# Gated embedding of a float32 encoder block: the last round of weight splits moved from GpSimd to VectorE, two squares left to the small matmuls, and one set of diagonals issued later

## The chip, the cores and the metric

One core of one Trainium2 chip. The metric is the device time of one execution, in microseconds (us): 2531.17 us for the kernel before, the median of three runs (2530.97 to 2533.29). Below, PE is TensorE (matmuls), DVE is VectorE, ACT is ScalarE, POOL is GpSimd, SP is the engine that issues most DMAs.

## The reference

The whole block has two SwiGLU half steps, two token mixers, a gated embedding and a final norm, on 1024 tokens of 1024 channels. Only its end matters here:

```python
ple_gate = jax.nn.sigmoid(rmsnorm(h, ple_norm[layer]) @ ple_w_gate[layer])
h = h + ple_gate * (p[layer] @ ple_w_proj[layer])
return rmsnorm(h, final_norm)
```

`ple_w_gate` is 1024 x 1024, `ple_w_proj` is 256 x 1024, `p` is 1024 x 256, everything in float32.

## The kernel before

**Layout.** Channels lie on the 128 partitions, tokens along the row. `h` is 8 blocks (`j`) of 128 channels by 1024 tokens, held as two halves of 512 tokens (`hsrc`, tile `r`). A float32 product is made of three passes of 32-bit "r" matmuls: each operand is split into `hi` (ACT copies and rounds, L98 for weights) and `lo` (the rest, a subtraction, L99), and `mm3` (L355) sums hi x hi, hi x lo and lo x hi.

**Weights.** `Weights` streams each 128 x 1024 unit of weights by DMA into one of four raw buffers (`wraw`, L80) and splits its two halves into one of seven slots (`wsplit`). A slot comes free when the unit that used it is done (`done`), and the next half is split at once (`ahead`). The subtraction L99 runs on the engine given to `plan`, on POOL where none is given.

**The embedding (`ple`).** The tokens are three pieces: piece 0 is tokens 0 to 511, piece 1 tokens 512 to 767, piece 2 tokens 768 to 1023. The first round (r = 0) goes through all eight blocks with pieces 0 and 1. The last round (r = 1) goes through the blocks from 7 down to 0 with piece 2 alone, and streams the gate weights of blocks 5 to 0 (and one unit of `ple_w_proj`) a second time; those of blocks 7 and 6 are kept.

A unit (one block, one piece; L1600 to L1626) is 24 gate matmuls and 6 projection matmuls on PE, then a chain: DVE L1614 (times the norm factor), ACT L1615 (sigmoid), DVE L1616 (times the projection), DVE L1618 (added into `h`), ACT L1624 (square), and one addition L1626 into the piece's sum of squares, on DVE in the last round.

**The final norm (`final`).** Per piece: `factors` sums the squares over the partitions with one small matmul per 128 tokens (L1639) and runs eleven tiny DVE instructions of a reciprocal square root (L373 to L379); `spread` makes a diagonal matrix per 128 tokens on DVE (L1650), multiplies it by ones on PE (L1651) and copies the result out of PSUM on ACT (L1653); `apply` scales each of the eight blocks, on DVE (L1668), or for blocks 1 and 5 on ACT and POOL (L1665, L1666), and stores it.

**The order.** Engines work their own queues in order. The norms of pieces 0 and 1 run inside the last round: `self.queue` holds their steps, and `tick`, called after every 8 gate matmuls (so three times per unit), takes one step from it, or counts down a number that stands there. A step's instructions are pinned behind what its engines had been given by then (`paced`). The norm of piece 2 comes after the last unit, with nothing beside it.

Of the kernel before, what the change touches and what calls it, by code (L numbers as in the profile page):

```python
# [9 lines left out]
ALU = mybir.AluOpType  # L10

P = 128
# [199 lines left out]
class Block:  # L212
# [1351 lines left out]
    def ple_plan(self):  # L1564
        io = self.io
        o = []
        for j in range(8):
            o.append((("ple", 0, j), io["ple_w_gate"][j]))
            if j % 4 == 0:
                o.append((("proj", 0, j // 4), io["ple_w_proj"][j // 4]))  # L1570
        for j in reversed(range(8 - PLE_KEPT)):
            o.append((("ple", 1, j), io["ple_w_gate"][j]))
            if j == 3:
                o.append((("proj", 1, 0), io["ple_w_proj"][0]))
        self.w.plan(o)

    def ple_keys(self, r, j):

# [14 lines left out]
    def ple(self):  # L1593

        nc, w = self.nc, self.w
        v = nc.vector
        io = self.io
        accs = {}
        pool = self.arena(4, 5)
        sums = pool.tile([P, 2, HALF], F32, name="accs")  # L1600
        pieces = [(0, 0, HALF), (1, 0, 256), (1, 256, HALF)]

        def unit(r, j, piece):
            h, a, b = pieces[piece]
            n = b - a
            gate, proj = self.ple_keys(r, j)
            wt = w.unit(gate)
            pg, ps = self.psum()[:, 0:n], self.psum()[:, 0:n]
            self.mm3(pg, [wt[k] + tuple(x[:, a:b] for x in self.x(k, h)) for k in range(KB)], ticks=8)
            cols = slice(h * HALF + a, h * HALF + b)  # L1610
            wp = w.unit(proj)
            self.mm3(ps, [wp[2 * (j % 4) + k] + (self.ph[:, k, cols], self.pl[:, k, cols]) for k in range(2)])
            s = self.t()[:, 0:n]
            v.tensor_tensor(out=s, in0=pg, in1=self.rs[:, h, a:b], op=ALU.mult)  # L1614
            nc.scalar.activation(s, s, AF.Sigmoid)  # L1615
            v.tensor_tensor(out=s, in0=s, in1=ps, op=ALU.mult)  # L1616
            d = self.hsrc(j, h)[:, a:b]
            v.tensor_tensor(out=d, in0=d, in1=s, op=ALU.add)  # L1618
            if piece not in accs:
                accs[piece] = sums[:, h, a:b]  # L1620
                nc.scalar.activation(accs[piece], d, AF.Square)
            else:
                sq = self.t()[:, 0:n]
                nc.scalar.activation(sq, d, AF.Square)  # L1624
                e = v if r or j == 7 else nc.gpsimd
                e.tensor_tensor(out=accs[piece], in0=accs[piece], in1=sq, op=ALU.add)  # L1626

        def final(piece):

            h, a, b = pieces[piece]  # L1630
            n = b - a
            nb = n // P
            rs = pool.tile([P, n], F32, tag="frs%d" % piece, name="frs")
            cols = iter([pool.tile([P, nb], F32, tag="f%d_%d" % (piece, i), name="fc") for i in range(3)])

            def factors():
                ps = self.aux()
                for c in range(nb):
                    nc.tensor.matmul(ps[:, c:c + 1], accs[piece][:, c * P:(c + 1) * P], self.ones[:, 0:1],  # L1639
                                     start=True, stop=True)  # L1640
                col = next(cols)
                self.rsqrt_mean(col, ps[:, 0:nb], D, lambda: next(cols))
                accs["col", piece] = col

            def spread():
                col = accs["col", piece]
                ps = self.aux()
                for c in range(nb):
                    dg = self.t()[:, 0:P]
                    v.tensor_scalar(out=dg, in0=self.ident, scalar1=col[:, c:c + 1], scalar2=None, op0=ALU.mult)  # L1650
                    nc.tensor.matmul(ps[:, c * P:(c + 1) * P], self.ones, dg, start=True, stop=True)  # L1651
                accs["rs", piece] = ps[:, 0:n]
                nc.scalar.activation(rs, ps[:, 0:n], AF.Copy)  # L1653

            def apply(j):
                g = self.gain["final_norm"][:, j:j + 1]
                if piece < 2:
                    o = self.t()[:, 0:n]
                else:
                    if j == 0:  # L1660
                        accs["o"] = pool.tile([P, KB, n], F32, name="fo")
                    o = accs["o"][:, j, :]
                d = self.hsrc(j, h)[:, a:b]
                if j % 4 == 1:
                    nc.scalar.activation(d, d, AF.Copy, scale=g)  # L1665
                    nc.gpsimd.tensor_tensor(out=o, in0=d, in1=rs, op=ALU.mult)  # L1666
                else:
                    v.scalar_tensor_tensor(out=o, in0=d, scalar=g, in1=accs["rs", 2] if piece == 2 else rs,  # L1668
                                           op0=ALU.mult, op1=ALU.mult)
                if piece < 2:  # L1670
                    nc.sync.dma_start(out=io["out"][j, :, h * HALF + a:h * HALF + b], in_=o)
                elif j % 2:
                    (nc.sync if j % 4 == 1 else nc.scalar).dma_start(
                        out=io["out"][j - 1:j + 1, :, h * HALF + a:h * HALF + b].rearrange("j p t -> p j t"),
                        in_=accs["o"][:, j - 1:j + 1, :])
            return [factors, spread] + [lambda j=j: apply(j) for j in range(KB)]

        for r in range(2):
            if r:
                f0, f1 = final(0), final(1)  # L1680
                self.queue = [1, f0[0], 1, f0[1], f1[0], f0[2], f0[3], f1[1]] + f0[4:] + f1[2:]
                for j in reversed(range(8)):
                    unit(r, j, 2)
                    gate, proj = self.ple_keys(r, j)
                    w.done(gate)
                    if j % 4 == 0:
                        w.done(proj)
                continue
            for j in range(8):
                if j == 0:  # L1690
                    unit(r, 0, 0)
                    unit(r, 1, 0)
                if j > 1:
                    unit(r, j, 0)
                unit(r, j, 1)
                if j < 8 - PLE_KEPT:
                    w.done(("ple", r, j))
                if j == 3:
                    w.done(("proj", r, 0))
        self.flush()  # L1700
        for f in final(2):
            f()
# [143 lines left out]
```

## Time and profile before

| what | value |
|---|---|
| median of three runs | 2531.17 us |
| the profiled execution's own time | 2530.26 us |
| its span, first to last instruction | 2528.1 us |
| PE busy | 2445.2 us (97%) |
| DVE busy | 1902.9 us (75%) |
| ACT busy | 908.4 us (36%) |
| POOL busy | 854.8 us (34%) |
| mean granted clock of TensorE | 0.986 |

The sum of the prediction is made against the profiled execution, which took 0.91 us less than the median. The busy shares are means over the whole program. The change touches only its last 83 us or so, so the views below are cut to that stretch: the table of stages (with the granted clock), the waits, and the timeline of each engine.

### The profile page before, as it was taken

The page shows a single profiled execution, that of the slowest core. Times are in us where ns is not written, and L with a number is a line of the kernel's source. Part 1 is how long each engine was busy: PE and PEld are TensorE (multiplying, and loading weights), DVE is VectorE, ACT ScalarE, POOL GpSimd, SP SyncE. Part 2 cuts the span into 40 slices and gives each one's busy share as a digit, 9 for nine tenths or more (in the row PEclk, how much of TensorE's full clock was granted, in tenths as well). Part 3 has the DMA queues.
Part 4 walks back from the last instruction along what each step waited for, and adds up shares of the span by engine and source line. Part 5 has one row for each costly group of instructions (what it writes and reads, how often), then busy time and mean ns, then how long its engine had stood idle before and what let it go on. Part 6 is the DMA issues. An engine that isn't in the chain of part 4 may idle for free. (4 is left out here: it accounts for less than half of the span.)

```text
span 2528.1 us, 34047 instructions
## 1 busy us (share of the span) xinstructions
PE 2445.2 (97%) x12128; PEld 2062.2 (82%) x12128; DVE 1902.9 (75%) x3043; ACT 908.4 (36%) x1594; POOL 854.8 (34%) x588
## 2 busy tenths in 40 slices
PE   8999998999999999999999899999999999999996
PEld 7888787788887888988889788787888888788886
DVE  8889999657787875685686478926889998658636
ACT  4322232445533443213213324323332333445523
POOL 4255454300137554112011113641255555200143
PEclk9999999999999999999999999999999999999998
DMA  4255554867423444213312335442256564866212
GB/s 163 84 205 200 188 200 165 292 227 220 160 67 120 132 149 145 73 51 73 87 51 64 111 103 189 140 137 71 92 192 212 195 231 169 314 203 211 68 59 92
DMA packets 195371, 373.30 MB, mean 148 GB/s; under 512 B 34913, under 2 KB 49505, under 8 KB 195169
## 3 DMA queue, kind: packets, MB, share of 16 engines
q1 hardware_dynamic: 194512, 370.57, 44.2%
q8 instruction: 96, 1.57, 0.3%
q14 instruction: 75, 0.61, 0.1%
q10 hardware_dynamic: 688, 0.55, 0.1%
HBM read 257.48 MB, written 113.57 MB: 147 GB/s over the span
## 5 line engine op out<-in xcount | busy, mean ns | idle before, releaser
L355 PE MATMUL mm<-q,wsplit 128*128 128x512 f32 (+1 forms) x7452 | 1693.6, 387 | 15.3 <-ACT wsplit L98 7.8
L355 PEld LDWEIGHTS mm<-q,wsplit 128*128 128x128 f32 x7452 | 1379.0, 190 | 299.0 <-ACT wsplit L98 9.9
L99 POOL TENSOR_TENSOR wsplit<-wraw,wsplit 128x512 fp32r<-128x512 f32 x368 | 531.5, 1457 | 1142.5 <-PE mm L732 388.9
L732 PE MATMUL mm<-wsplit 128*128 128x512 f32 x1848 | 422.8, 391 | 5.5 <-DVE wsplit L347 3.7
L98 ACT ACTIVATE wsplit<-wraw 128x512 fp32r<-128x512 f32 x464 | 281.5, 626 | 372.2 <-PE mm L355 173.5
L732 PEld LDWEIGHTS mm<-wsplit 128*128 128x128 f32 x1848 | 347.5, 188 | 79.0 <-DVE wsplit L347 4.6
L347 DVE TENSOR_TENSOR wsplit<-space,wsplit 128x512 fp32r<-128x512 f32 x308 | 207.8, 712 | 131.8 <-PE mm L732 93.3
L346 ACT ACTIVATE wsplit<-space 128x512 fp32r<-128x512 f32 x308 | 192.6, 633 | 204.6 <-PE mm L732 168.0
L119 DVE TENSOR_TENSOR wraw<-wraw 128x512 f32<-128x512 f32 x153 | 154.3, 1008 | 48.9 <-POOL wsplit L99 44.9
L559 DVE TENSOR_TENSOR t<-t,mm 128x512 f32<-128x512 f32 x252 | 167.8, 677 | 0.0
L612 DVE TENSOR_TENSOR r<-r 128x512 f32<-128x512 f32 x120 | 150.9, 1257 | 6.9 <-DMA r<-in_ffn_w_down_dram 6.1
L99 POOL TENSOR_TENSOR wsplit<-t,wsplit 128x512 fp32r<-128x512 f32 x51 | 84.8, 1662 | 202.1 <-ACT wsplit L98 168.8
L99 DVE TENSOR_TENSOR wsplit<-wraw,wsplit 128x512 fp32r<-128x512 f32 x96 | 114.5, 1200 | 11.5 <-PE mm L355 7.4
L1226 PEld LDWEIGHTS mm<-space,space 128*128 128x128 f32 x896 | 108.0, 194 | 17.3 <-issue 6.3
L1226 PE MATMUL mm<-space,space 128*128 128x64 f32 x896 | 109.1, 274 | 12.0 <-DVE space L1233 6.8
L98 ACT ACTIVATE wsplit<-t 128x512 fp32r<-128x512 f32 x51 | 32.3, 634 | 233.8 <-DVE t L119 204.4
L355 PE MATMUL mm<-wsplit,q 128*128 128x256 f32 x768 | 100.3, 286 | 0.0
L529 POOL TENSOR_TENSOR a<-a 128x512 f32<-128x512 f32 x44 | 73.3, 1667 | 68.2 <-DVE a L550 46.1
L355 PEld LDWEIGHTS mm<-wsplit,q 128*128 128x128 f32 x768 | 94.2, 191 | 0.1
L562 ACT ACTIVATE t<-t 128x512 f32<-128x512 f32 x72 | 45.6, 634 | 134.5 <-DVE t L559 134.5
L1354 DVE TENSOR_TENSOR t<-t,mm 128x512 f32<-128x512 f32 x107 | 70.9, 678 | 23.5 <-PE mm L355 9.6
L1232 DVE TENSOR_TENSOR space<-space 128x512 f32<-128x512 f32 x48 | 35.1, 731 | 69.5 <-PE mm L1226 69.5
(255 smaller groups left out, 2048.0 us busy)
## 6 DMA issues: line engine op xcount, KB each, us to landing
space<-ffn_act SPq DMA_DIRECT2D x154, 256.0 KB, 3.2
ffn_act<-a SPq DMA_DIRECT2D x110, 256.0 KB, 5.5
wraw<-in_ffn_w_gate_dram SPq DMA_DIRECT2D x44, 512.0 KB, 3.3
wraw<-in_ffn_w_up_dram SPq DMA_DIRECT2D x44, 512.0 KB, 4.2
r<-in_ffn_w_down_dram SPq DMA_DIRECT2D x22, 1024.0 KB, 6.2
ffn_sums<-r SPq DMA_DIRECT2D x22, 1024.0 KB, 6.4
wraw<-in_w_in_dram SPq DMA_DIRECT2D x44, 512.0 KB, 3.9
space<-ffn_sums SPq DMA_DIRECT2D x88, 256.0 KB, 2.7
```

What stands on the lines that cost most here:

```text
L98: self.nc.scalar.activation(hi, src, AF.Copy)
L99: engine.tensor_tensor(out=lo, in0=src, in1=hi.bitcast(F32), op=ALU.subtract)
L119: sub = lambda out, x, y: v.tensor_tensor(out=out, in0=x, in1=y, op=ALU.subtract)
L346: self.nc.scalar.activation(hi, src, AF.Copy)
L347: lo_engine.tensor_tensor(out=lo, in0=src, in1=hi.bitcast(F32), op=ALU.subtract)
L355: self.last = nc.tensor.matmul(ps, al if p == 2 else ah, bl if p == 1 else bh, start=p == order[0] and i == 0, stop=p == order[2] and i == ...
L529: g.tensor_tensor(out=x[n], in0=x[a], in1=x[b], op=op)
L559: add = lambda out, x, y: v.tensor_tensor(out=out, in0=x, in1=y, op=ALU.add)
L612: v.tensor_tensor(out=room[:, out, :], in0=room[:, x, :], in1=room[:, y, :], op=ALU.subtract)
L732: self.last = nc.tensor.matmul(ps[j], a[:, j * P:(j + 1) * P], b, start=p == 0 and m == 0, stop=p == NP - 1 and m == 2)
L1226: nc.tensor.matmul(ps[:, c * 64:(c + 1) * 64].rearrange("p (b i) -> p b i", i=h), K[:, c * HC:(c + 1) * HC], q3[:, c * cb:(c + 1) * cb, :] ...
L1354: add = lambda o, x, y: nc.vector.tensor_tensor(out=o, in0=x, in1=y, op=ALU.add)
```

## The change

Five edits, all in `ple_plan` and `ple`:

1. The weights of the last round are planned with `engine = nc.vector`: their 14 subtractions L99 stand on DVE, none on POOL.
2. The scaling of blocks 1 and 5 of pieces 0 and 1 is DVE's (L1668), where it was ACT's and POOL's. Piece 2 keeps ACT and POOL for them.
3. The squares of the last two units (blocks 1 and 0 of piece 2) are not added by DVE; they are kept, and the small matmuls of piece 2's `factors` sum three tiles where they summed one.
4. The step that makes piece 0's diagonals stands behind a countdown of three ticks after its factors, where the countdown was one.
5. The step that makes piece 1's diagonals stands behind three of piece 0's scalings and a countdown of two, where it stood behind two scalings.

```diff
@@ ple_plan
+        self.w.plan(o)
+        o = []
         for j in reversed(range(8 - PLE_KEPT)):
             o.append((("ple", 1, j), io["ple_w_gate"][j]))
             if j == 3:
                 o.append((("proj", 1, 0), io["ple_w_proj"][0]))
-        self.w.plan(o)
+        self.w.plan(o, self.nc.vector)
@@ ple
-        accs = {}
+        accs = {"more": []}
@@ unit
-                e = v if r or j == 7 else nc.gpsimd
-                e.tensor_tensor(out=accs[piece], in0=accs[piece], in1=sq, op=ALU.add)
+                if r and j < 2:
+                    accs["more"].append(sq)
+                else:
+                    e = v if r or j == 7 else nc.gpsimd
+                    e.tensor_tensor(out=accs[piece], in0=accs[piece], in1=sq, op=ALU.add)
@@ factors
+                parts = [accs[piece]] + (accs["more"] if piece == 2 else [])
                 for c in range(nb):
-                    nc.tensor.matmul(ps[:, c:c + 1], accs[piece][:, c * P:(c + 1) * P], self.ones[:, 0:1],
-                                     start=True, stop=True)
+                    for i, x in enumerate(parts):
+                        nc.tensor.matmul(ps[:, c:c + 1], x[:, c * P:(c + 1) * P], self.ones[:, 0:1],
+                                         start=i == 0, stop=i == len(parts) - 1)
@@ apply
-                if j % 4 == 1:
+                if j % 4 == 1 and piece == 2:
@@ last round
-                self.queue = [1, f0[0], 1, f0[1], f1[0], f0[2], f0[3], f1[1]] + f0[4:] + f1[2:]
+                self.queue = [1, f0[0], 3, f0[1], f1[0], f0[2], f0[3], f0[4], 2, f1[1]] + f0[5:] + f1[2:]
```

Lines of the changed kernel stand lower: L1616, L1618, L1620 and L1631 there are L1614, L1616, L1618 and L1626 of the kernel before, L1646 is L1639, L1657 is L1650, L1658 is L1651, L1675 is L1668.

**DVE around the second pair of diagonals** (those of piece 1). Before:

```order
L1668 SCALAR_TENSOR_TENSOR t<-r_66,gains,space_18290 128x512
L1614 TENSOR_TENSOR t<-mm,rs 128x256
L1616 TENSOR_TENSOR t<-t,mm 128x256
L1618 TENSOR_TENSOR r_66<-r_66,t 128x256
L1626 TENSOR_TENSOR space_18290<-space_18290,t 128x256
L1650 TENSOR_SCALAR t<-ident,space_18290 128x128 x2
L1668 SCALAR_TENSOR_TENSOR t<-r_66,gains,space_18290 128x512
```

Changed:

```order
L99 TENSOR_TENSOR wsplit<-wraw,wsplit 128x512
L1620 TENSOR_TENSOR r_66<-r_66,t 128x256
L99 TENSOR_TENSOR wsplit<-wraw,wsplit 128x512
L1631 TENSOR_TENSOR space_18290<-space_18290,t 128x256
L1675 SCALAR_TENSOR_TENSOR t<-r_66,gains,space_18290 128x512
L1616 TENSOR_TENSOR t<-mm,rs 128x256
L99 TENSOR_TENSOR wsplit<-wraw,wsplit 128x512
L1618 TENSOR_TENSOR t<-t,mm 128x256
L99 TENSOR_TENSOR wsplit<-wraw,wsplit 128x512
L1620 TENSOR_TENSOR r_66<-r_66,t 128x256
L1657 TENSOR_SCALAR t<-ident,space_18290 128x128 x2
L1675 SCALAR_TENSOR_TENSOR t<-r_66,gains,space_18290 128x512
```

From the first tiny instruction of piece 0's factors to these two diagonals, DVE's queue now holds 12 of the splits L99, the 22 tiny instructions of both chains, four diagonals of piece 0, fourteen instructions of units (four each of L1614, L1616, L1618 and two of L1626) and three scalings L1668; before it held none of the splits and one scaling.

**PE around the product with these diagonals** (`q` and `space_16585` are the operands of gate and projection). Before, it comes 24 gate matmuls after the projection of block 6, ahead of that of block 5:

```order
L355 MATMUL mm<-q_16687,wsplit 128x256 x4
L1651 MATMUL mm<-t,ones 128x128 x2
L355 MATMUL mm<-space_16585,wsplit 128x256 x6
L355 MATMUL mm<-q_16686,wsplit 128x256 x4
L355 MATMUL mm<-q_16687,wsplit 128x256 x4
```

Changed, it comes two units later, ahead of the projection of block 3:

```order
L355 MATMUL mm<-q_16686,wsplit 128x256 x4
L355 MATMUL mm<-q_16687,wsplit 128x256 x4
L1658 MATMUL mm<-t,ones 128x128 x2
L355 MATMUL mm<-space_16585,wsplit 128x256 x6
L355 MATMUL mm<-q_16686,wsplit 128x256 x4
L355 MATMUL mm<-q_16687,wsplit 128x256 x4
```

Behind it on PE stand 96 matmuls of 256 columns. The product with piece 0's four diagonals comes 38 such matmuls after the small matmuls of its factors, where it came 27 after; the small matmuls of piece 1's factors stand 14 matmuls behind it, where they stood 3 behind it; and 76 matmuls lie between those and the product with piece 1's diagonals.

**PE at the very end**, after the last unit. Before:

```order
L355 MATMUL mm<-q_16687,wsplit 128x256 x4
L355 MATMUL mm<-space_16585,wsplit 128x256 x6
L1639 MATMUL mm<-ones,space_18290 128x1 x2
L1651 MATMUL mm<-t,ones 128x128 x2
L1841 UNCONDITIONAL_BRANCH
```

Changed:

```order
L355 MATMUL mm<-space_16585,wsplit 128x256 x6
L1646 MATMUL mm<-ones,space_18290 128x1
L1646 MATMUL mm<-ones,t 128x1 x2
L1646 MATMUL mm<-ones,space_18290 128x1
L1646 MATMUL mm<-ones,t 128x1 x2
L1658 MATMUL mm<-t,ones 128x128 x2
L1848 UNCONDITIONAL_BRANCH
```

Two small matmuls have become six, of which the last four wait for the square of block 0. A float32 matmul of this table is two in the profile.

## Rows read from the trace of the kernel before

**Rows 1.** Stages of the end: busy time (instructions) per engine, granted clock, DMA.

```profile
core 0: us, PE busy (x) PEld busy (x) DVE busy (x) ACT busy (x) POOL busy (x), PEclk, DMA share, GB/s
2467.40:2482.10 14.70, 12.67 (x106) 12.26 (x104) 11.13 (x33) 4.91 (x10) 5.08 (x4) 1.00 0.20 71
2482.10:2493.70 11.60, 6.54 (x34) 6.28 (x35) 9.40 (x14) 5.21 (x12) 5.38 (x5) 0.71 0.32 115
2493.70:2509.10 15.40, 15.36 (x129) 15.16 (x127) 11.81 (x16) 5.46 (x13) 11.99 (x9) 1.00 0.32 119
2509.10:2516.70 7.60, 0.00 (x0) 0.00 (x1) 5.06 (x13) 2.59 (x6) 0.00 (x0) 0.75 0.20 69
```

**Rows 2.** Waits from 2465 to 2529: us in total, times, longest.

```profile
PE mm L1651 <- DVE t L1650: 9.6, 4, 4.7
```

**Rows 3.** Timeline, PE: start, us, instruction, count, idle before and releaser.

```profile
2469.28 0.95 PE L1639 MATMUL mm<-ones,space 128*128 128x1 f32 x8
...
2475.56 1.16 PE L1651 MATMUL mm<-t,ones 128*128 128x128 f32 x8 [1.99 <-DVE t L1650]
...
2486.79 0.77 PE L1651 MATMUL mm<-t,ones 128*128 128x128 f32 x2 [4.73 <-DVE t L1650]
...
2489.81 4.14 PE L355 MATMUL mm<-q,wsplit 128*128 128x256 f32 x24
...
2504.59 0.88 PE L355 MATMUL mm<-space,wsplit 128*128 128x256 f32 x6
...
2508.18 0.88 PE L355 MATMUL mm<-space,wsplit 128*128 128x256 f32 x6
```

**Rows 4.** Timeline, DVE and POOL in the last round.

```profile
2470.95 2.54 POOL L99 TENSOR_TENSOR wsplit<-wraw,wsplit 128x512 fp32r<-128x512 f32 x2 [11.05 <-PE mm L355]
...
2471.06 1.20 DVE L379 SCALAR_TENSOR_TENSOR space<-space 128x4 f32<-128x4 f32 x1
...
2485.37 2.51 DVE L1650 TENSOR_SCALAR t<-ident,space 128x128 f32<-128x128 f32 x2
...
2497.82 4.91 DVE L1668 SCALAR_TENSOR_TENSOR t<-r,gains,space 128x512 f32<-128x512 f32 x3
```

**Rows 5.** Timeline of the end: the last unit and piece 2's factors.

```profile
2513.96 0.42 DVE L1614 TENSOR_TENSOR t<-mm,rs 128x256 f32<-128x256 f32 x1
...
2515.31 0.42 DVE L1618 TENSOR_TENSOR r<-r,t 128x256 f32<-128x256 f32 x1
...
2516.22 0.43 DVE L1626 TENSOR_TENSOR space<-space,t 128x256 f32<-128x256 f32 x1 [0.48 <-ACT t L1624]
...
2516.70 1.01 PE L1639 MATMUL mm<-ones,space 128*128 128x1 f32 x4 [7.64 <-DVE space L1626]
2517.75 0.16 DVE L373 TENSOR_SCALAR space<-mm 128x2 f32<-128x2 f32 x1 [1.10 <-PE mm L1639]
...
2519.91 0.48 DVE L1650 TENSOR_SCALAR t<-ident,space 128x128 f32<-128x128 f32 x2
```

**Rows 6.** Timeline, DVE: prices of a split, of diagonals and of scalings.

```profile
2149.24 0.69 DVE L99 TENSOR_TENSOR wsplit<-wraw,wsplit 128x512 fp32r<-128x512 f32 x1
2149.84 0.68 DVE L559 TENSOR_TENSOR t<-t,mm 128x512 f32<-128x512 f32 x1
...
2475.22 0.87 DVE L1650 TENSOR_SCALAR t<-ident,space 128x128 f32<-128x128 f32 x4
...
2492.09 1.41 DVE L1668 SCALAR_TENSOR_TENSOR t<-r,gains,space 128x512 f32<-128x512 f32 x2
...
2510.16 0.87 DVE L1668 SCALAR_TENSOR_TENSOR t<-r,gains,space 128x256 f32<-128x256 f32 x2
```

**Rows 7.** Timeline, PE, an earlier wait of like length.

```profile
2177.77 4.62 PE L732 MATMUL mm<-wsplit 128*128 128x512 f32 x12 [2.90 <-DVE wsplit L347]
```

**Rows 8.** The stage around that earlier wait, columns as in rows 1.

```profile
2174.00:2182.00 8.00, 5.09 (x16) 3.68 (x15) 8.00 (x9) 1.63 (x3) 4.86 (x3) 0.79 0.53 191
```

**Rows 9.** The page's costliest groups: splits on DVE, whole program: busy, mean ns, idle.

```profile
L99 DVE TENSOR_TENSOR wsplit<-wraw,wsplit 128x512 fp32r<-128x512 f32 x96 | 114.5, 1200 | 11.5 <-PE mm L355 7.4 <-ACT wsplit L98 2.6 <-POOL t L389 1.6
```

## The prediction

> **What bounds the kernel now.** I read the table of stages first. From 2467.4 to 2482.1 PE is busy 12.67 of 14.70 us, then 6.54 of 11.60 at a mean granted clock of 0.71, then full until 2509.1, then idle for 7.6 us while DVE still works [rows 1]. So the last round is bound twice over: PE stalls in its middle, and after PE's last matmul DVE has a backlog to clear.
>
> The list of waits names the stalls: PE's product L1651 waited four times, 9.6 us in all, for DVE's diagonals L1650, once for 4.7 us [rows 2]. On PE's timeline the first is 1.99 us at 2475.56 and the second 4.73 us at 2486.79. Behind the second the granted clock is halved: (1 - 0.71) / 0.5 x 11.6 = 6.7 us of that stage run at 1.2 instead of 2.4 GHz [rows 1], and 24 gate matmuls took 4.14 us there. At full clock a whole unit of 30 matmuls passes in 2508.18 - 2504.59 = 3.6 us, or 0.12 us each [rows 3].
>
> Why DVE is late stands on its own timeline. While POOL subtracts weights, a DVE instruction with operands in SBUF hangs until POOL's ends: a tiny L379 took 1.20 us beside POOL's two L99, the two diagonals took 2.51 us, three scalings 4.91 us [rows 4]. Without POOL the eleven tiny steps take 2519.91 - 2517.75 = 2.16 us, all of them. The last unit then reaches DVE at 2513.96, 2513.96 - 2509.06 = 4.9 us after PE had ended (2508.18 + 0.88), its last addition L1618 ends at 2515.73, and from there a serial tail runs to the end [rows 5].
>
> **The change, part by part.** Until 2470.23, where the four small matmuls of piece 0's factors end (2469.28 + 0.95 [rows 3]), only one of the 14 moved splits has come; it lies where PE is 100% busy and DVE is not, so it costs nothing. I follow both queues from there.
>
> *Splits and scalings to DVE.* A split starts 2149.84 - 2149.24 = 0.60 us before its neighbour, though it lasts 0.69. A scaling of 512 tokens costs 0.70 (1.41 / 2), one of 256 tokens 0.44, four diagonals 0.87 [rows 6], any unit instruction 0.42 [rows 5]. From DVE's first tiny step to the second pair of diagonals the changed queue holds two chains of 2.16 (4.3), 12 splits (7.2), 14 unit instructions (5.9), six diagonals (1.3) and three scalings (2.1): 20.8 us. POOL is silent, so none of these hangs. DVE starts them at about 2470.27 and has the first of the two diagonals at 2490.9.
>
> *Diagonals later.* Piece 0's come after one chain, two splits, three unit instructions and one diagonal: 2.16 + 1.2 + 1.26 + 0.3 = 4.9, at 2475.2. PE has 38 matmuls first, 4.6 us, and is there at 2474.8: it waits 0.4 us instead of 1.99. It goes on with that product (1.16 [rows 3]), 14 matmuls (1.7), four small instructions (0.5) and 76 matmuls (9.1), and stands before piece 1's diagonals at 2487.7. It waits 3.2 us, until 2490.9, instead of 4.73. So this stall is shorter, not gone: the splits that freed DVE from POOL now stand ahead of the diagonals.
>
> *The rest of PE.* Two products at 0.29 (1.16 / 4) and 96 matmuls: 0.6 + 11.5, to 2503.0 at full clock. What 3.2 us of idling do to the clock has no row of its own length; the nearest is a wait of 2.90 us [rows 7], and the stage around it had (1 - 0.79) / 0.5 x 8.0 = 3.4 us at half clock [rows 8]. The wait of 1.99 us cost no clock at all (1.00 in its stage [rows 1]) and that of 4.73 cost 6.7 us of it. I take 3.4, the nearest row, which delays the work by half of it, 1.7 us; the bounds are 0 and 3.4. PE ends at 2504.7, against 2509.06.
>
> *DVE behind it.* Up to the last L1616 it has five scalings of 512 (3.5), six of 256 (2.6), three L1626 (1.3), ten unit instructions (4.2) and one split (0.6): 12.2 us, from 2491.1 to 2503.3. That is inside PE's 2504.7, with 1.4 us to spare, so the backlog is gone: the last L1616 goes at 2504.8, L1618 ends 0.9 later, at 2505.7. Before, it ended at 2515.73: **10.0 us gained**. Of these, PE's end gives 4.4 and the backlog the rest. ACT loses four scalings, and POOL keeps two instructions of the last round; both were off the path.
>
> *The squares.* After L1618 the square L1624 is as before. The sum then cost L1626 and two small matmuls: 2516.70 - 2516.22 = 0.48, and 1.01 at half clock [rows 5]. Now four small matmuls, eight instructions, wait for the square: 0.12 each at full clock (0.95 / 8 [rows 3]), 0.96 in all; at half clock 1.9. PE has idled only about a microsecond by then, less than the 1.99 that cost no clock, so I take full clock: 0.5 gained (0.4 lost at the other end). The two L1626 that go save DVE nothing at PE's pace.
>
> *Other edits.* The DMAs of the last three units of weights wait for splits on DVE instead of POOL. In the sum these splits come earlier than POOL's did, as POOL's last ones ran in the stage from 2493.7 on [rows 1]; so the loads come no later. On SP's queue all of them now stand ahead of the stores, one of which stood before the last load.
>
> **Sum:** 10.5 us off the profiled 2530.26, 2519.8. The median of the runs is 0.91 above the profiled one, so the forecast for the median is 2531.17 - 10.5 = **2520.7 us**.
>
> *A rule weighed.* The rows show a split's neighbour starting 0.09 us before the split has ended [rows 6]. The Trainium skill (VectorE: DVE Perf Modes, The DRAIN you can't avoid) says that the next DVE instruction does not start until the pipeline of the one before is empty. By that rule each split would cost 0.69, and the trace speaks against it; what it would make of the time is the second rival.
>
> **Rivals.**
>
> *No clock is lost.* If the chains' tiny steps slip in between splits, the 3.2 us of waiting shrink by about 1 us to near 2, the length that cost no clock. Then 1.0 + 1.7 more is gained: 2518.0. For it: the chain's steps stand between independent entries in the order, and each needs DVE for only 0.16 of its 0.2 us. Against it: the additions of so many entries leave no slack for waits on ACT that I have not counted.
>
> *DVE is slower than summed, and sets the pace again.* If nothing on DVE overlaps, 12 splits cost 0.09 more each and scalings 0.04, 1.2 us ahead of the diagonals. The stall is 4.4, close to the 4.73 that cost 6.7 us of half clock, so 1.7 more is lost: 2520.7 + 1.2 + 1.7 = 2523.6. With another microsecond or two of waits for ACT (each unit crosses to ACT and back) it is 2525. This is also the shape in which the diagonals "later" don't help: PE waits as long, two units on. The skill's section gives the splits' part of it. For it: a queue served in order, with waits for ACT inside. Against: the rows' overlap, and that other entries fill those waits.
>
> *The splits are slow in themselves.* The page gives 1200 ns as their mean on DVE [rows 9]. If that is not POOL's doing, 12 of them cost 7.2 us more before the diagonals, a stall of over 10 us and at least 3.4 more of clock: 0 gained, 2531. Against it: 0.69 at 2149.24 with POOL off [rows 6].
>
> *PE starves for weights: slower.* The `lo` half of a unit's weights now waits behind unit instructions that themselves wait for PE. If the queues lock step, a unit takes its PE time (3.6) plus two splits, its four DVE instructions and a scaling (1.2 + 1.7 + 0.7 = 3.6) one after the other: 7.2 for each of six units, 21.6 more, 2520.7 + 21.6 = 2542. It decides as soon as a split is queued later than PE's third pass over that unit. In the sum the last split goes at about 2496 and PE's third pass of block 0 is near 2503, so 7 us would have to go wrong. To be 5 us slower than before, each unit would have to lose 2.6 us.
>
> **How the numbers follow.** A measurement of this kernel can tell about 0.2%, 5.1 us, from no change. Forecast (gain of 9 to 12): 0.55. No clock lost: 0.16. DVE sets the pace: 0.19. Splits slow in themselves: 0.07. Starved: 0.03. The first three are faster by more than 5.1 us but for a tail of the third (0.01): faster 0.89. No change 0.08, slower 0.03. The range takes in the first three, from half a microsecond below the first rival to half a microsecond above the end of the second: 2517.5 to 2525.5. It leaves out the last two cases and the tails.
>
> **What would show it.** Right: POOL without L99 after 2450; L379 at 0.16 throughout; one PE wait for diagonals of about 3 us near 2488, and one of under 1 us near 2475; 3.4 us of half clock behind it; PE ending near 2505 and L1618 about 1 us after it; twelve small-matmul records at the end, at 0.12 each. Wrong: a stall of 5 us or more, splits on DVE over 0.8 us, PE waiting for `wsplit` from DVE, or DVE's last unit still microseconds behind PE.

## The result, and the profile after

The changed kernel takes **2518.46 us** (median of five runs, 2516.18 to 2521.98), where the kernel before took 2530.97 beside it (five runs, 2529.11 to 2533.29). The ratio is **0.9949**, with an interval of [0.9938, 0.9959]: 12.9 us of 2531 are gone. The forecast of 2520.7 lies 2.2 us above the median, inside its range.

The page of the profiled execution (2518.29 us on its own) has, for the span and the busy times:

```profile
span 2516.5 us, 34051 instructions
...
PE 2444.2 (97%) x12136; PEld 2060.3 (82%) x12136; DVE 1898.0 (75%) x3059; ACT 905.0 (36%) x1590; POOL 829.8 (33%) x570
```

The busy shares are those of before; POOL alone lost something that shows (25 us).

**A common starting point.** Up to the four small matmuls of piece 0's factors the two programs differ in one of the 14 moved splits alone, yet these start at 2469.28 in the trace of before [rows 3] and at 2470.73 in that of after; in the twelve traces of this study they start anywhere from 2466.60 to 2472.77. I therefore measure everything below **from the start of these small matmuls**. From there to the end of the span before took 2528.1 - 2469.28 = 58.8 us, and after takes 2516.5 - 2470.73 = 45.8: **13.06 us less** (the spans alone differ by 11.6, as this execution came to that point 1.45 later).

The stages of after, to be held against [rows 1] (the columns are those of [rows 1]):

```profile
2470.73:2476.18 5.45, 5.45 (x49) 5.45 (x48) 4.60 (x20) 2.60 (x6) 0.00 (x0) 1.00 0.28 96
2476.18:2488.50 12.32, 12.28 (x104) 12.07 (x102) 11.73 (x34) 7.14 (x15) 0.00 (x0) 1.00 0.37 129
2488.50:2490.90 2.40, 0.00 (x0) 0.03 (x1) 2.40 (x8) 0.89 (x3) 0.00 (x0) 1.00 0.28 109
2490.90:2503.00 12.10, 12.10 (x102) 12.10 (x102) 10.98 (x26) 4.08 (x10) 0.00 (x0) 1.00 0.39 144
2503.00:2516.50 13.50, 2.72 (x17) 2.25 (x16) 6.53 (x24) 1.22 (x3) 1.23 (x2) 0.65 0.37 126
```

PE is full but for one hole of 2.4 us, and **the granted clock is 1.00 in the hole and behind it**, where before it was 0.71 in the stage with the hole. POOL is silent until the tail. DVE is busy for nearly all of the hole and for 11.73 of 12.32 us ahead of it: in this stretch it has become the full engine.

From the list of waits of after (us in total, times, longest), against [rows 2]:

```profile
PE mm L1658 <- DVE t L1657: 5.0, 2, 2.5
```

Of the four waits two are left: the hole, and the one in the tail. The timeline of PE, against [rows 3] and [rows 5]:

```profile
2470.73 0.95 PE L1646 MATMUL mm<-ones,space 128*128 128x1 f32 x8
...
2476.18 1.05 PE L1658 MATMUL mm<-t,ones 128*128 128x128 f32 x8
...
2490.90 0.68 PE L1658 MATMUL mm<-t,ones 128*128 128x128 f32 x4 [2.45 <-DVE t L1657]
...
2492.14 3.04 PE L355 MATMUL mm<-q,wsplit 128*128 128x256 f32 x24
...
2502.22 0.88 PE L355 MATMUL mm<-space,wsplit 128*128 128x256 f32 x6
...
2505.05 0.38 PE L1646 MATMUL mm<-ones,t 128*128 128x1 f32 x2 [1.61 <-ACT t L1626]
2505.30 0.36 PE L1646 MATMUL mm<-ones,space 128*128 128x1 f32 x2
2505.52 0.58 PE L1646 MATMUL mm<-ones,t 128*128 128x1 f32 x4
```

The first product with diagonals has no wait at all, the second one of 2.45 us; the 24 matmuls behind it take 3.04 us, full clock, where [rows 3] had 4.14. And the timeline of DVE, against [rows 4] and [rows 5]:

```profile
2471.72 0.16 DVE L373 TENSOR_SCALAR space<-mm 128x4 f32<-128x4 f32 x1 [0.56 <-PE mm L1646]
...
2473.38 0.15 DVE L379 SCALAR_TENSOR_TENSOR space<-space 128x4 f32<-128x4 f32 x1
2473.45 0.69 DVE L99 TENSOR_TENSOR wsplit<-wraw,wsplit 128x512 fp32r<-128x512 f32 x1
...
2481.50 0.15 DVE L379 SCALAR_TENSOR_TENSOR space<-space 128x2 f32<-128x2 f32 x1
2481.57 0.69 DVE L99 TENSOR_TENSOR wsplit<-wraw,wsplit 128x512 fp32r<-128x512 f32 x1
2482.17 0.15 DVE L377 TENSOR_TENSOR space<-space 128x2 f32<-128x2 f32 x1
2482.24 0.69 DVE L99 TENSOR_TENSOR wsplit<-wraw,wsplit 128x512 fp32r<-128x512 f32 x1
...
2488.27 0.42 DVE L1616 TENSOR_TENSOR t<-mm,rs 128x256 f32<-128x256 f32 x1
2488.60 0.68 DVE L99 TENSOR_TENSOR wsplit<-wraw,wsplit 128x512 fp32r<-128x512 f32 x1
...
2490.47 0.48 DVE L1657 TENSOR_SCALAR t<-ident,space 128x128 f32<-128x128 f32 x2
2490.86 0.75 DVE L1675 SCALAR_TENSOR_TENSOR t<-r,gains,space 128x512 f32<-128x512 f32 x1
...
2502.77 0.42 DVE L1616 TENSOR_TENSOR t<-mm,rs 128x256 f32<-128x256 f32 x1
...
2504.13 0.42 DVE L1620 TENSOR_TENSOR r<-r,t 128x256 f32<-128x256 f32 x1
```

L379 takes 0.15 us where it took 1.20. A tiny step that stands between two splits costs next to nothing: the split behind it starts 0.07 us after it. The last addition L1620 ends at 2504.55, 33.8 us from the common start, where before it ended at 46.5. The tail behind it is about as long as it was, 11.95 us against 12.37. So nearly all of the gain, 12.6 of 13.1 us, was made ahead of the last addition.

### The profile page after: what moved, and what is told of

The parts are those of the page before. It is cut to its first block, busy times and chain, and to the rows that moved or that the text cites. A ratio compares the mean times of both kernels' runs of the same rounds, so it can differ in the third digit from the quotient of the medians.

```text
span 2516.5 us, 34051 instructions
## 1 busy us (share of the span) xinstructions
PE 2444.2 (97%) x12136; PEld 2060.3 (82%) x12136; DVE 1898.0 (75%) x3059; ACT 905.0 (36%) x1590; POOL 829.8 (33%) x570
## 3 DMA queue, kind: packets, MB, share of 16 engines
q1 hardware_dynamic: 194512, 370.57, 44.2%
## 5 line engine op out<-in xcount | busy, mean ns | idle before, releaser
L99 POOL TENSOR_TENSOR wsplit<-wraw,wsplit 128x512 fp32r<-128x512 f32 x354 | 511.6, 1458 | 1112.9 <-PE mm L732 387.4
L99 POOL TENSOR_TENSOR wsplit<-t,wsplit 128x512 fp32r<-128x512 f32 x51 | 84.2, 1652 | 204.5 <-ACT wsplit L98 150.4
L99 DVE TENSOR_TENSOR wsplit<-wraw,wsplit 128x512 fp32r<-128x512 f32 x110 | 122.4, 1119 | 11.6 <-PE mm L355 7.4
L1226 PE MATMUL mm<-space,space 128*128 128x64 f32 x896 | 109.2, 274 | 12.9 <-DVE space L1233 7.6
```

The costliest lines, as they stand in the source:

```text
L99: engine.tensor_tensor(out=lo, in0=src, in1=hi.bitcast(F32), op=ALU.subtract)
L1226: nc.tensor.matmul(ps[:, c * 64:(c + 1) * 64].rearrange("p (b i) -> p b i", i=h), K[:, c * HC:(c + 1) * HC], q3[:, c * cb:(c + 1) * cb, :] ...
```

## The experiments

Ten kernels ran, three groups on three chips. All measure the same few places, so one table holds them: microseconds from the start of the small matmuls of piece 0's factors in each kernel's trace; the wait is that of PE for piece 1's diagonals, and the stretch at half clock is the one by that wait. The last column is the ratio to the kernel before on the same chip, with its interval.

| kernel | wait for the 2nd diagonals | half clock by it | PE's last projection ends | last addition ends | end of span | ratio |
|---|---|---|---|---|---|---|
| before | 4.73 | 6.83 | 39.8 | 46.5 | 58.8 | 1 |
| after | 2.45 | 0 | 32.4 | 33.8 | 45.8 | 0.9949 [0.9938, 0.9959] |
| e1_pool_out | 3.63 | 6.83 | 36.5 | 39.4 | 51.5 | 0.9967 [0.9956, 0.9977] |
| e2_queue | 8.22 | 6.83 | 41.2 | 45.2 | 57.8 | 0.9994 [0.9985, 1.0004] |
| e3_squares_back | 2.45 | 0 | 32.4 | 34.7 | 46.9 | 0.9957 [0.9940, 0.9973] |
| e6_queue_back | 3.63 | 6.83 | 36.3 | 38.4 | 50.4 | 0.9962 [0.9949, 0.9975] |
| e4_splits_pool | 7.89 | 6.83 | 40.6 | 44.2 | 57.0 | 0.9988 [0.9978, 0.9997] |
| e5_scaling_pool | 3.30 | 6.83 | 35.9 | 37.0 | 48.9 | 0.9948 [0.9931, 0.9964] |
| e7_stall_longer | 4.18 | 3.41 | 35.8 | 36.9 | 48.9 | 0.9956 [0.9941, 0.9970] |
| e8_diag_first | none | 0 | 29.7 | 33.9 | 46.7 | 0.9948 [0.9933, 0.9963] |
| e9_four_squares | none | 0 | 29.7 | 32.6 | 44.5 | 0.9937 [0.9924, 0.9949] |
| e10_pool_busy | 5.96 | 6.83 | 39.6 | 42.8 | 55.1 | 0.9978 [0.9969, 0.9987] |

The intervals of neighbours overlap, as the runs of one kernel spread by 3 to 12 us; which edit did what is read from one trace of each, with the ratios as a check. Each run went the way that its first theory said, but some sizes in the table lie outside what was expected: e1 gained less (7.3 us, 8 to 11 expected), as did e4 (1.8; 2 to 5); e6 cost more (4.6; 2 to 4), as did e5 (3.2; at most 2.7) and, by 0.2, e8 (0.9; at most 0.7); e7 cost less (3.1; 4 or more).

**e1_pool_out: edits 1 and 2 alone (POOL out of the last round), old queue, squares as before.**

```diff
-        self.w.plan(o)
+        self.w.plan(o, self.nc.vector)
...
-                if j % 4 == 1:
+                if j % 4 == 1 and piece == 2:
```

> The kernel before with edits 1 and 2 alone: splits and scalings of the last round on VectorE, GpSimd silent; diagonals and squares as they were. Theory A (a silent GpSimd is most of the gain, since VectorE no longer hangs behind it): 8 to 11 us faster than before; one PE wait for piece 1's diagonals of about 3.5 us, about 10 us behind the small matmuls of piece 0's factors; tiny steps at 0.16 us. Rival B (the later diagonals are most of it): under 4 us faster, with a PE wait of 5 us or more.

It gives 58.8 - 51.5 = **7.3 us**, over half of the whole. With the old queue the second diagonals are asked for one unit and a bit after piece 0's (10.9 us from the start, against 17.7), PE waits 3.63 us, and the clock falls. The row of its timeline of PE:

```profile
2484.51 1.19 PE L1653 MATMUL mm<-t,ones 128*128 128x128 f32 x4 [3.63 <-DVE t L1652]
```

And its stretch at half clock (columns as in [rows 1], so in all such rows below):

```profile
2483.47:2490.30 6.83, 5.79 (x27) 5.82 (x28) 5.26 (x12) 1.74 (x4) 0.00 (x0) 0.50 0.37 142
```

**e2_queue: edits 4 and 5 alone (the new queue, POOL still splits).**

```diff
-                self.queue = [1, f0[0], 1, f0[1], f1[0], f0[2], f0[3], f1[1]] + f0[4:] + f1[2:]
+                self.queue = [1, f0[0], 3, f0[1], f1[0], f0[2], f0[3], f0[4], 2, f1[1]] + f0[5:] + f1[2:]
```

> The kernel before with edits 4 and 5 alone: diagonals later, GpSimd still splits and scales. Theory A: within 2 us of before on either side, because VectorE hangs behind GpSimd anyway and the wait for piece 1's diagonals comes back two units later, at 5 to 9 us. Rival B: 6 us faster or more, with no PE wait over 2 us.

Alone the new queue is worth 1.0 us, and no difference can be told in the runs (0.9994). The first stall shrinks to 0.67 us, but the second grows to 8.22: asked for later, the diagonals are later still, since DVE's queue ahead of them hangs beside POOL. PE's rows:

```profile
2475.65 1.16 PE L1651 MATMUL mm<-t,ones 128*128 128x128 f32 x8 [0.67 <-DVE t L1650]
...
2496.26 0.77 PE L1651 MATMUL mm<-t,ones 128*128 128x128 f32 x2 [8.22 <-DVE t L1650]
```

**e3_squares_back: the change without edit 3.**

```diff
-                if r and j < 2:
+                if False:
```

> The changed kernel without edit 3: VectorE adds all squares again. Theory A: 0.5 to 1.6 us slower than the changed kernel (two additions on VectorE of 0.42 us, less two small matmuls per column at the end), so 11 to 12 us faster than before. Rival (the squares carry the gain): 4 us or more slower than the changed kernel.

PE runs as in after, to a tenth of a microsecond (the same 2.45 us wait, the last projection ends at 32.4), and the end comes 46.92 - 45.77 = **1.15 us** later. Of that 0.90 stand ahead of the last addition, where DVE has an addition more and waits 0.48 us for its square, and 0.25 in the tail.

**e6_queue_back: the change with the old queue.** The edit is e2's, backwards, on the changed kernel.

> The changed kernel without edits 4 and 5: diagonals where they were. Theory A: the diagonals are due 7 us earlier on PE, the wait for them is 3.5 us instead of 2.45, and, if a wait of that length halves the granted clock, 3.4 us of half clock follow: 2 to 4 us slower than the changed kernel, 9 to 11 us faster than before. Rival B: 8 us or more slower than the changed kernel.

50.38 against 45.77: the queue is worth **4.6 us** with POOL silent, and the 3.63 us wait of e1 is back, to the hundredth. e1 to e6 is the squares once more (1.13), e1 to e3 the queue once more (4.6). So the parts add up: 7.32 (POOL out) + 1.13 (squares) + 4.61 (queue) = 13.06. Most of the queue's part exists only once POOL is out: alone it was 1.0 (e2).

**e4_splits_pool: the change with the splits back on POOL.**

```diff
-        self.w.plan(o, self.nc.vector)
+        self.w.plan(o)
```

> The changed kernel with the last round's splits back on GpSimd (edit 1 undone, the rest kept). Theory A: VectorE hangs behind 13 GpSimd splits again and the wait for piece 1's diagonals is 5 to 9 us: only 2 to 5 us faster than before. Rival B: 8 us or more faster than before.

11.2 us are lost again, and the wait is 7.89. The splits on POOL are enough for it; that the scalings are DVE's doesn't help.

**e5_scaling_pool: the change with the scalings of blocks 1 and 5 back on ACT and POOL.**

```diff
-                if j % 4 == 1 and piece == 2:
+                if j % 4 == 1:
```

> The changed kernel with the scalings of blocks 1 and 5 of pieces 0 and 1 back on ScalarE and GpSimd (edit 2 undone). Theory A: VectorE loses 2.1 us of work but hangs behind four GpSimd scalings of 0.9 to 1.4 us: within 2.7 us of the changed kernel, on the slower side. Rival (VectorE's load alone counts, not GpSimd's): 2 us faster than the changed kernel.

In its trace the wait is 3.30 us instead of 2.45, with POOL busy for 1.26 us of it, and 6.83 us of half clock follow; the end is 3.2 us later. The row of PE's timeline:

```profile
2493.80 1.20 PE L1658 MATMUL mm<-t,ones 128*128 128x128 f32 x4 [3.30 <-DVE t L1657]
```

The stage of the wait, and the stretch at half clock:

```profile
2490.50:2493.80 3.30, 0.00 (x0) 0.03 (x1) 3.27 (x7) 1.36 (x4) 1.26 (x1) 0.87 0.20 79
...
2492.92:2499.75 6.83, 5.95 (x28) 5.98 (x29) 4.43 (x9) 1.68 (x4) 0.66 (x1) 0.50 0.40 154
```

But the ratio, 0.9948, is that of the change. The profiled run was the longest of the four (2523.49 us, mean clock 0.986), and the other three, at 0.989, took 2514.80 to 2521.19. Whether the wait cost those any clock their traces would have to tell, which I don't have. So edit 2 is worth 3.2 us in the one execution seen and nothing that can be told in the median; that stays open.

**e7_stall_longer: the change, with four multiplications by one behind each of piece 1's diagonals.** No value changes; only the wait grows.

```diff
+                    for _ in range(4 if piece == 1 else 0):
+                        v.tensor_tensor(out=dg, in0=dg, in1=self.ones, op=ALU.mult)
```

> The changed kernel with piece 1's two diagonals multiplied by ones four times each (8 more VectorE instructions of 128 columns between the diagonals and PE's product, values unchanged). The wait for them grows from 2.45 us to 4 us or more. If a longer wait halves the granted clock: 3.4 to 6.8 us of 0.5 behind it, PE's matmuls after it end 1.7 to 3.4 us later on top of the longer wait, 4 us or more slower than the changed kernel. If the clock plays no part: slower by the added VectorE work alone, about 2.4 us.

The wait is 4.18 us, 1.73 more, and 3.41 us of PE's work behind it run at half clock, which costs 1.7: PE ends 3.45 later, the sum of the two, and the span 3.1 later. The clock's fall is no part of the wait itself here: it comes 0.36 us after PE has gone on (2488.51). The row of PE's timeline, then the wait and the stretch at half clock in the table of stages:

```profile
2488.51 1.24 PE L1660 MATMUL mm<-t,ones 128*128 128x128 f32 x4 [4.18 <-DVE t L1659]
```

```profile
2484.33:2488.50 4.17, 0.00 (x0) 0.03 (x1) 4.17 (x15) 1.04 (x3) 0.00 (x0) 1.00 0.16 63
2488.87:2492.28 3.41, 3.41 (x16) 3.34 (x16) 2.80 (x7) 1.04 (x3) 0.00 (x0) 0.50 0.40 154
```

**e8_diag_first: the change, with piece 1's diagonals made right behind its factors and kept for the product.** This asks which engine sets the pace of the change: if PE's stall does, taking it away must move the last addition; if DVE's queue does, it must not.

```diff
+                if piece == 1:
+                    accs["dg"] = [self.t()[:, 0:P] for _ in range(nb)]
+                    for c, dg in enumerate(accs["dg"]):
+                        v.tensor_scalar(out=dg, in0=self.ident, scalar1=col[:, c:c + 1], scalar2=None, op0=ALU.mult)
...
-                    dg = self.t()[:, 0:P]
-                    v.tensor_scalar(out=dg, in0=self.ident, scalar1=col[:, c:c + 1], scalar2=None, op0=ALU.mult)
+                    if piece == 1:
+                        dg = accs["dg"][c]
+                    else:
+                        dg = self.t()[:, 0:P]
+                        v.tensor_scalar(out=dg, in0=self.ident, scalar1=col[:, c:c + 1], scalar2=None, op0=ALU.mult)
```

> The changed kernel with piece 1's two diagonals made right behind their chain of tiny steps instead of ahead of PE's product. The wait of 2.45 us should go. Theory D (VectorE's queue sets the pace from there on, PE's wait is slack): within 0.7 us of the changed kernel, PE idle instead before the last small matmuls. Rival C (PE's wait is on the path): 2 to 2.5 us faster than the changed kernel.

The wait is gone, and PE's last projection ends 2.7 us earlier (29.7 against 32.4). The last addition does not move: 33.9 against 33.8. So **DVE's queue sets the pace, and taking away the 2.45 us hole of the change gains nothing**. It is later than PE by little, though: in after the last L1616 starts 0.55 us after the last projection has begun (2502.77, 2502.22), and in e7, where it waits for PE, 0.20 after (2501.73, 2501.53). A hole longer by more than about 0.35 us (the difference, an estimate) puts PE back on the path, as e5 and e7 did. From its timeline, PE's end and DVE's last unit:

```profile
2485.24 0.60 PE L1665 MATMUL mm<-t,ones 128*128 128x128 f32 x4
...
2498.39 0.88 PE L355 MATMUL mm<-space,wsplit 128*128 128x256 f32 x6
...
2501.73 0.42 DVE L1616 TENSOR_TENSOR t<-mm,rs 128x256 f32<-128x256 f32 x1
...
2503.09 0.42 DVE L1620 TENSOR_TENSOR r<-r,t 128x256 f32<-128x256 f32 x1
...
2504.90 0.99 PE L1646 MATMUL mm<-ones,t 128*128 128x1 f32 x4
```

DVE takes up the last unit 3.3 us after its gate matmuls have ended (2498.39, where the projection begins). PE then idles before the last small matmuls, and they run at half clock, the last four in 0.99 us where after has four in 0.58; the tail is 0.8 us longer. So the time is no better for it.

**e9_four_squares: e8, and the squares of four units left to the small matmuls instead of two.** If DVE sets the pace, two additions fewer must show.

```diff
-                sq = self.t()[:, 0:n]
+                sq = pool.tile([P, n], F32, name="sq") if r and j < 4 else self.t()[:, 0:n]
...
-                if r and j < 2:
+                if r and j < 4:
...
-                for c in range(nb):
-                    for i, x in enumerate(parts):
+                for i, x in enumerate(parts):
+                    for c in range(nb):
                         nc.tensor.matmul(ps[:, c:c + 1], x[:, c * P:(c + 1) * P], self.ones[:, 0:1],
-                                         start=i == 0, stop=i == len(parts) - 1)
+                                         start=i == 0 and c == 0, stop=i == len(parts) - 1 and c == nb - 1)
```

> The changed kernel with piece 1's diagonals made behind their chain, the squares of the last four units (not two) left to the small matmuls, and those matmuls ordered tile by tile, so that only the last two (not four) wait for the last square. Theory D (VectorE's queue sets the pace): two additions less, the last addition into h ends 0.7 us earlier after the small matmuls of piece 0's factors than in the changed kernel (33.8 us), and the tail loses 0.5 us more, unless it falls to half clock: 0.3 to 1.3 us less than the changed kernel's 45.8 us from those matmuls to the end. Rival (PE's extra small matmuls set the end): no shorter, or longer by up to 1 us.

They show, and by more than was expected (0.7 us against the change): the last addition ends 1.35 us earlier than in e8 (32.57 against 33.92) and 1.25 earlier than in the change, and the end comes 2.2 earlier, 1.27 earlier than the change (44.50 against 45.77). With the loops turned round, sixteen of the twenty small matmuls pass while DVE works on the last unit, and only four wait for the last square:

```profile
2501.44 1.84 PE L1646 MATMUL mm<-ones,space 128*128 128x1 f32 x16
2505.00 1.01 PE L1646 MATMUL mm<-ones,space 128*128 128x1 f32 x4 [1.71 <-ACT space L1626]
```

Its median is 2517.27 us (five runs, 2516.03 to 2519.64), its ratio 0.9937 [0.9924, 0.9949]. It beats the kernel before clearly; that it beats the change is seen in the trace and is too small for the intervals.

**e10_pool_busy: the change, with four multiplications on POOL per unit whose result nothing reads.** 24 of them, 17.8 us of POOL's time. This is to part two readings of e1: that DVE waited for POOL's results, or that it hangs because POOL works at all.

```diff
+            if r and j > 1:
+                for _ in range(4):
+                    nc.gpsimd.tensor_tensor(out=junk, in0=d, in1=d, op=ALU.mult)
```

> The changed kernel with GpSimd made to do useless work in the last round: after each of the first six units four squarings of that unit's h (128 x 256, both operands and the result in SBUF, result unused), some 17 us in all; nothing waits for them. Theory A (VectorE's instructions with SBUF operands hang while GpSimd's run): tiny steps, splits and scalings last up to 0.7 us longer when they meet one; the stretch from the small matmuls of piece 0's factors to the end grows from 45.8 to 50 us or more. Rival (GpSimd's mere work costs nothing; what cost was waiting for its splits): 45.8 within 0.7 us, VectorE's durations unchanged.

The end comes **9.4 us later** (55.1 against 45.8), though nothing reads what POOL makes, and most of the gain in the runs is gone (0.9978). The wait for the second diagonals is 5.96 us and the half clock is back. From its timeline, beside POOL's first four:

```profile
2472.70 2.75 POOL L1624 TENSOR_TENSOR space<-r 128x256 f32<-128x256 f32 x4 [14.03 <-DVE space L379]
2472.73 0.60 DVE L377 TENSOR_TENSOR space<-space 128x4 f32<-128x4 f32 x1
...
2473.56 0.46 DVE L379 SCALAR_TENSOR_TENSOR space<-space 128x4 f32<-128x4 f32 x1
2474.06 1.66 DVE L1661 TENSOR_SCALAR t<-ident,space 128x128 f32<-128x128 f32 x4
```

A tiny step takes 0.60 or 0.46 us and four diagonals 1.66, where [rows 6] have 0.87. Over the whole stretch the additions L1635 take 727 ns on the mean (420 in after) and the scalings of 512 tokens 965 (748); L1617 and L1619, which read one operand from PSUM, keep their length (412 and 419, against 419 and 420). The Trainium skill (SBUF — State Buffer, Who interferes with whom) says that a VectorE instruction with two inputs in SBUF contends with a GpSimd instruction that reads SBUF, and that in the two-port modes one of them blocks for the whole of the other. The durations here agree with the first part.

The run doesn't part the two readings wholly, for one instruction does wait for POOL. ACT's L1676 scales block 5 of `h` in place, and has to wait until POOL has read it; the sigmoid L1618 stands behind it on ACT, and DVE waits for that just ahead of the second diagonals:

```profile
2490.93 0.51 ACT L1676 ACTIVATE r<-r,gains 128x256 f32<-128x256 f32 x1 [2.40 <-POOL space L1624]
...
2491.78 0.42 DVE L1619 TENSOR_TENSOR t<-t,mm 128x256 f32<-128x256 f32 x1 [1.35 <-ACT t L1618]
```

The second diagonals start 24.7 us from the common start (2493.06), where after has 19.7 (2490.47). Of these 5.0 us up to 1.35 come of that wait, and the rest of DVE's longer instructions. So the 9.4 us are not all the price of hanging: this wait and the half clock are in them.

## Why the prediction was right, and where it was off

**The splits on DVE, without POOL: right.** The 13 splits of this stretch take 0.686 us on the mean, no L379 hangs, POOL does nothing. The groups of DVE from 2466 to 2518 in after (busy, mean ns, idle), against the 1200 of [rows 9]:

```profile
L99 DVE TENSOR_TENSOR wsplit<-wraw,wsplit 128x512 fp32r<-128x512 f32 x13 | 8.9, 686 | 0.1
```

So the rival of splits that are slow in themselves falls. So does the one of PE starving: PE waits for no weights behind the common start. e10 shows the reason given (DVE hangs because POOL works), by the lengths of DVE's instructions, rather than leaving it to fit.

**The way from the small matmuls to the second diagonals: 20.8 us was too long.** DVE was through with the two diagonals 2490.86 - 2471.72 = 19.1 us after its first tiny step. Counted from start to start, two terms were mis-sized by about as much. The "two chains of 2.16 (4.3)" took 3.5: between independent entries a tiny step costs 0.07 us of DVE's queue (2481.50 to 2481.57), in a row still 0.2. That is the condition of the rival **"No clock is lost"**. "14 unit instructions (5.9)" took 4.9: an instruction of 0.42 us costs about 0.33 where the next entry is independent, as with L1616 at 2488.27 and the split at 2488.60. So tiny steps and unit instructions overlap too, where the sum allowed that to splits and scalings only. The splits took 7.4, for 7.2.

The other rival's price, DVE instructions that don't overlap, is spoken against: the tiny L377 at 2482.17 starts 0.60 us after a split that lasts 0.69. The Trainium skill's rule that was weighed there (VectorE: DVE Perf Modes, The DRAIN you can't avoid) would have it start 0.69 after it, but the same section adds that a next instruction that is not held starts earlier, and this trace agrees with that addition.

**The stalls.** Piece 0's: forecast 0.4 us, found none. Piece 1's: forecast 3.2, found 2.45, as the diagonals came 1.5 us sooner and PE 0.7 sooner than summed.

**The half clock: this step failed.** "I take 3.4, the nearest row, which delays the work by half of it, 1.7 us": it was 0. With the shorter wait that is the rival's 2518.0, and the median is 2518.46. So what came is the rival that was given 0.16, not the forecast, and the range held because it took that rival in. e3 shows the same 2.45 us wait without loss; e5 (3.30), e1 and e6 (3.63) and e7 (4.18) show longer ones with 6.83, 6.83 and 3.41 us at half clock. So a somewhat longer wait does cost what the forecast feared. That 2.45 us cost nothing is shown for two traces only, and may be luck: in e5 the clock fell 2.42 us after PE had stopped (2492.92 - 2490.50), sooner than the wait of after was over.

**The pace behind it: wrong in the engine.** "That is inside PE's 2504.7, with 1.4 us to spare." The sum for DVE came out, 12.2 us forecast and 2503.19 - 2490.95 = 12.2 found from the end of the diagonals to the end of the last L1616 of after (L1614 of before), where that sum stops. It holds two waits for ACT, 1.0 us, that the forecast left out and that the overlap of other instructions makes up. But PE's last projection ends 3.0 us sooner than forecast (32.4 from the start, against 2504.7 - 2469.28 = 35.4), with 1.7 of the clock and 1.2 of the two stalls. With that, DVE is the later of the two, by about 0.35 us, and e8 shows it. "The two L1626 that go save DVE nothing at PE's pace" falls with it: they save 0.90 us there (e3), and the tail 0.25, so edit 3 is worth 1.15 and not 0.5.

**The sum.** Forecast: 10.0 at the last addition and 0.5 in the tail. Found: 12.6 and 0.4. Nearly all of the 2.6 us between is the clock (1.7) and the shorter waits (1.2), less the half microsecond that DVE's last unit is late.

## What to carry to other kernels

Where a chain of short VectorE steps holds up TensorE, look first at what GpSimd does beside it: taking its work away gave 7.3 us of the span here (e1), though VectorE, the busier engine, had to do it instead, and work that nothing needed cost 9.4 (e10, a wait of ScalarE for it included). An edit of the order may be worth nothing until another edit frees the engine that it waits on (1.0 us and then 4.6 for the same queue), so such edits are tried together as well as alone. And before a stall of the bounding engine is attacked, let it end earlier in a trial: in e8 taking 2.45 us of it away did not bring the last addition forward at all.

## What the runs showed of the hardware that was not expected

- **The clock does not go by the length of a wait alone.** The 2.45 us wait of after was followed by a granted clock of 1.00. Far ahead of it, in the same trace, a shorter one was followed by 0.50; the row of PE's timeline, and the stage behind it:

```profile
1339.66 3.57 PE L1226 MATMUL mm<-space,space 128*128 128x64 f32 x16 [2.36 <-DVE space L1233]
```

```profile
1342.00:1346.00 4.00, 4.00 (x13) 3.42 (x13) 1.92 (x3) 1.24 (x3) 1.81 (x1) 0.50 0.02 4
```

  At the second diagonals the clock fell 2.59 us (e1), 2.42 us (e5) and 4.54 us (e7) after PE had stopped: in the first two PE still idled, in the third it already worked again. In e5 that is sooner than the wait of after was over (2.45 us), where the clock didn't fall. These runs don't tell what else it goes by.

- **The same work reaches the same place at different times.** The small matmuls of piece 0's factors start within 6.2 us of each other in the twelve traces, though next to nothing ahead of them differs. A gain of a microsecond is seen only from a common point in the trace.
